# Softmax denominators of an attention stage: through memory as rows, in place of TensorE transposes

## The chip, the cores and the metric

The kernel runs on one core of one Trainium2 chip. The metric is the device time of one execution in microseconds (us), taken as the median of several runs. The engines are named as the profile names them: PE (TensorE, with PEld for its weight loads), DVE (VectorE), ACT (ScalarE), POOL (GpSimd) and SP (SyncE, which here issues nearly all DMAs).

## What is computed

Two layers of a trunk with 1024 latent tokens and 256 context tokens, D = 1024. Each layer projects the normalised input, runs three token mixers (retention with 4 heads, grouped-query attention with 6, latent attention "MLA" with 6), multiplies the concatenated heads by a SiLU gate and projects back:

```python
def block_attention(q, k, v, scale):      # gqa: 6 heads; mla: 6 heads, with a rotary part in q and k
    s = einsum('bqkgd,bskd->bkgqs', qi, k) * scale
    p = softmax(s, axis=-1)
    return einsum('bkgqs,bskd->bqkgd', p, v)

def _post(x, o_ret, o_gqa, o_mla, z_gate, g_res, w_out):
    y = concatenate([o_ret, o_gqa, o_mla], axis=-1) * silu(z_gate)
    return x + g_res * (y @ w_out)
```

The part at issue is the softmax's division by the sum of the exponentials, which the kernel does after the product with V, and the product with the gate.

## The kernel before, in words

All is float32, with operands of matmuls split into a high and a low part. Tokens lie in 10 tiles of 128 (8 latent, 2 context). A layer is a projection stage, an attention stage and an output projection. The attention stage is at about 520 to 1000 us in the first layer and 1570 to 2036 us in the second.

The attention stage works on pairs: `Pair(i, pr, mla)` is one head i (0 to 5) of one kind (mla 1, or grouped-query 0) and two neighbouring query tiles 2 pr and 2 pr + 1 (pr 0 to 4). There are 30 pairs of each kind per layer. Their order is the list `pairs` (L1391 to L1402): the grouped-query pair x, and the MLA pair x - 3, by turns. A latent pair (pr 0 to 3) has keys in 3 blocks of 512, a context pair (pr 4) one block of 256; each pair has a job per tile and block.

`advance` (L1365) is one step: it writes one s_job (scores, two or three matmuls, then a maximum on DVE), and, some steps later, exp_job (exponentials on ACT, with the row sums; after the last block DVE makes the reciprocals `ri`, L1277 to L1280), t_job (four transposes on PE, copied out by ACT and subtracted by DVE), and pv_job (products with V on PE, summed in one PSUM bank `o`, and added by DVE into the columns of the head, L1317). `clock` counts the steps. The result lies transposed: partition 64 mla + c is channel c of the head, and the free axis is the queries. Grouped-query heads fill partitions 0 to 63, MLA heads 64 to 127 of the same columns, `head_cols(p)` (L1326). The queries were in these columns before.

The reciprocals `ri` lie the other way, with queries on partitions: 128 x (2 tiles x 2 kinds). So `y_job` (L1350), which runs once when both kinds of a head and tile pair are done, copies them on POOL 64 times each into `rb` (L1355), transposes `rb` on PE into a PSUM bank of tag `tp` (L1358; these banks, two of them, serve t_job too), lets DVE multiply (L1359), and POOL multiply by the gates `gt` (L1360), which SP loaded from memory (L1335).

The program is laid out by a planner: the kernel writes instructions with priorities (`up(...)`), and the planner places them on each engine in order of its own estimate of readiness. Each engine then runs its list in order. SP's list holds all loads of the stage: the rotary queries `qst` (L1180, split by POOL into Qr), the gates, the staging `st` of K and V (L1086 to L1107, split by POOL, L192 and L193), and at the end the output weights (L223).

Of the kernel before, what the change touches and what calls it, by code (L numbers as in the profile page):

```python
# [10 lines left out]
F32 = mybir.dt.float32  # L11
# [3 lines left out]
ALU = mybir.AluOpType  # L15
# [3 lines left out]
P = 128  # L19
# [4 lines left out]
DEPTH = 2  # L24
# [52 lines left out]
SV = 0  # L77
WG = 1
PO = 1


def hybrid_trunk(tc, I, O):
# [3 lines left out]
    V, A, G, T = nc.vector, nc.scalar, nc.gpsimd, nc.tensor  # L86
    dma = nc.sync.dma_start
# [12 lines left out]
    s_mv = [tc.dram_tile([6 * P, NCH * 64], F32, name=f"s_mv{l}") for l in range(DEPTH)]  # L100
    s_kpT = [tc.dram_tile([NCH * 32, P], F32, name=f"s_kpT{l}") for l in range(DEPTH)]
    s_mt = [tc.dram_tile([P, 512], F32, name=f"s_mt{l}") for l in range(DEPTH)]
    s_gate = [tc.dram_tile([2, D], F32, name=f"s_gate{l}") for l in range(DEPTH)]


# [6 lines left out]
    ident = cst.tile([P, P], F32, name="ident")  # L112
# [21 lines left out]
    def bank(tag):  # L134
        if tag == "o":
            return pp.tile([P, 512], F32, name=tag, tag=tag, bufs=1)
        if tag == "m":
            tag = "tp"
        bufs = {"acc": NACC, "tp": 7 - NACC}[tag]
        return pp.tile([P, 512], F32, name=tag, tag=tag, bufs=bufs)  # L140

    def up(offset):
        return tc.high_priority(offset=offset) if offset else nullcontext()
# [297 lines left out]
    def phase_b(l, p1, acts, ws, first, first_side, first_done, att):  # L441
# [260 lines left out]
        blk(gqa_fn, post=side)  # L702
        blk(gqb_fn, post=side, posts=PO)
        for _ in side:
# [355 lines left out]
    def attention(l, att):  # L1060
# [3 lines left out]
        at = None  # L1064
# [174 lines left out]
        exps, trs, pvs, ys = [], [], [], []  # L1239
        clock = [0]  # L1240
# [27 lines left out]
        def exp_job(p, i, b, ps):  # L1268
            pn = at.tile([P, 512], F32, name="pn", tag="pn", bufs=PN)[:, :p.w]
            A.activation(pn, ps, AF.Exp, bias=p.ng[i], accum_out=p.su[:, i, b:b + 1])  # L1270
            p.pn[i, b] = pn
            if b == p.nb - 1 and i == 1:
                if (p.i, p.pr) not in ris:
                    ris[p.i, p.pr] = sm.tile([P, 2, 2], F32, name="ri", tag="ri", bufs=RB)
                ri = ris[p.i, p.pr][:, :, p.mla]
                if p.nb > 1:
                    V.tensor_reduce(ri, p.su[:, :, 0:p.nb], axis=AX.X, op=ALU.add)  # L1277
                    V.reciprocal(ri, ri)
                else:
                    V.reciprocal(ri, p.su[:, :, 0])  # L1280

        def t_job(p, i, b):
            if i == 0:
# [42 lines left out]
        def head_cols(p):  # L1326

            return yxs[:, 2 * p.pr:2 * p.pr + 2, Y_H + p.i * 128:Y_H + (p.i + 1) * 128]

        ris, halves, gates = {}, {}, {}  # L1330
# [8 lines left out]
        def gate_retention(p):  # L1339
# [5 lines left out]
            if p.i == 1:  # L1345
                rets.append((p.pr, at.tile([P, 2, 2, 128], F32, name="gr", tag="gr", bufs=1)))
                dma(rets[0][1].rearrange("p k t c -> p k (t c)"),
                    s_gT[l][0:Y_H, 2 * p.pr * P:(2 * p.pr + 2) * P].rearrange("(k p) c -> p k c", p=P))

        def y_job(p):  # L1350

            pm = bank("tp")[:, :256]
            ri = ris.pop((p.i, p.pr)).rearrange("p t s -> p (t s)")
            rb = at.tile([P, 256], F32, name="rb", tag="rb", bufs=1)
            G.tensor_scalar(rb.rearrange("p (x c) -> p x c", c=64), ri.unsqueeze(2).to_broadcast([P, 4, 64]), 1.0, 1.0,  # L1355
                            op0=ALU.mult, op1=ALU.mult)
            for i in range(2):
                T.transpose(pm[:, i * 128:(i + 1) * 128], rb[:, i * 128:(i + 1) * 128], ident)  # L1358
            V.tensor_tensor(head_cols(p), head_cols(p), pm.rearrange("p (t c) -> p t c", t=2), op=ALU.mult)  # L1359
            G.tensor_tensor(head_cols(p), head_cols(p), gates.pop((p.i, p.pr)), op=ALU.mult)  # L1360
            gate_retention(p)

        LAG_E, LAG_T, LAG_V = LE, LT, LV
# [1 line left out]
        def advance(jobs):  # L1365

            s = clock[0]
            if jobs is not None:
                with up(OS):
                    s_job(*jobs)  # L1370
            if exps and s >= LAG_E:
                with up(OE):
                    exp_job(*exps.pop(0))
            if trs and trs[0][0] <= s and (trs[0][2], trs[0][3]) in trs[0][1].pn:
                _, p, i, b = trs.pop(0)
                with up(OT):
                    t_job(p, i, b)
                if i == 1:
                    h = max(1, p.nch // HV)
                    pvs.append((s + LAG_V, p, b, 0, h))  # L1380
                    pvs.append((s + LAG_V + 1, p, b, h, p.nch))
            if pvs and pvs[0][0] <= s:
                with up(OV):
                    pv_job(*pvs.pop(0)[1:])
            if ys and ys[0][0] <= s:
                with up(OY):
                    y_job(ys.pop(0)[1])
            clock[0] += 1
# [3 lines left out]
        for x in range(30 + LEAD):  # L1392
            for mla, y in ((1, x - LEAD), (0, x)):
                if 0 <= y < 30:
                    p = Pair()
# [20 lines left out]
        for n, p in enumerate(pairs):  # L1416
# [7 lines left out]
            for u in range(2):  # L1424
                for b in range(p.nb):
                    if early[0] == 0:
                        yield "prepared"
                        at = att.ctx.enter_context(tc.tile_pool(name=f"at{l}", reuse_waits="tile", bufs=1))
# [18 lines left out]
                    if credit[0] >= 1:  # L1447
                        credit[0] -= 1
                        step()
        while exps or trs or pvs or ys:  # L1450
            advance(None)
        att.ctx.close()

# [239 lines left out]
```

## Time and profile before

| | us |
|---|---|
| median of 3 runs | 2163.22 (2162.13 to 2165.7) |
| the profiled execution | 2162.85 |
| its span | 2161.1 |
| PE busy | 2084.2 (96%) |
| PE weight loads busy | 1870.0 (87%) |
| DVE busy | 1502.0 (70%) |
| ACT busy | 1183.5 (55%) |
| POOL busy | 978.2 (45%) |

Busy shares are averages over stages of different kinds. A stage is read from its windows (busy time of each engine in a stretch), its waits (who stood idle for whom) and its timeline (instructions by start). Durations of matmuls overlap with their neighbours, so that the time a matmul takes of PE is better read from the start of the next one.

### The profile page before, as it was taken

Reading aid. Unit: us, or ns where it says so; the run is one execution under the profiler, and the core shown is the slowest. Engines: PE = TensorE matmul, PEld = TensorE weight load, DVE = VectorE, ACT = ScalarE, POOL = GpSimd, SP = SyncE. Lnnn points to the kernel's source line nnn. Section 1 sums busy time; section 2 is a strip of 40 time slices with the busy share of each in tenths; the row PEclk is TensorE's granted clock in tenths of the full one; section 3 lists DMA queues with packets and bytes.
Section 4 is the critical chain, followed back from the end, with each engine's and each line's share of the span. In section 5 each row is a group of like instructions: output and inputs, shape, how many; then the busy total and the mean of one; then the engine's idle time right before and its main releaser. Section 6 shows DMA issues by size and latency. Waiting matters only on the chain. (4 is left out here: it accounts for less than half of the span.)

```text
span 2161.1 us, 42292 instructions
## 1 busy us (share of the span) xinstructions
PE 2084.2 (96%) x14888; PEld 1870.0 (87%) x14888; DVE 1502.0 (70%) x3830; ACT 1183.5 (55%) x3180; POOL 978.2 (45%) x1444
## 2 busy tenths in 40 slices
PE   7999999999999999999999999998999999999998
PEld 3899987788888888888999999887788888888898
DVE  4625583666889999997174358546689899999824
ACT  3503333225788888886243233322488888888623
POOL 2341242315576465533543324233375656453474
PEclk8999999999999999999999999999999999999999
DMA  9542446414111010004143212452311111000322
GB/s 315 145 145 63 123 112 204 122 49 117 36 44 28 20 30 25 13 27 136 46 153 102 66 54 55 140 152 66 109 46 30 32 30 32 14 22 18 98 91 98
DMA packets 189117, 173.30 MB, mean 80 GB/s; under 512 B 35833, under 2 KB 171625, under 8 KB 188905
## 3 DMA queue, kind: packets, MB, share of 16 engines
q1 hardware_dynamic: 187464, 165.35, 25.7%
q10 hardware_dynamic: 1440, 5.24, 0.6%
q8 instruction: 119, 1.95, 0.4%
q14 instruction: 94, 0.76, 0.1%
HBM read 124.77 MB, written 45.76 MB: 79 GB/s over the span
## 5 line engine op out<-in xcount | busy, mean ns | idle before, releaser
L256 PE MATMUL acc<-wh,ah 128*128 128x256 f32 (+1 forms) x1760 | 503.4, 286 | 1.8 <-ACT ah L404 1.8
L258 PE MATMUL acc<-wh,al 128*128 128x256 f32 (+1 forms) x1760 | 500.6, 284 | 2.5 <-DVE al L405 2.4
L257 PE MATMUL acc<-wl,ah 128*128 128x256 f32 (+1 forms) x1760 | 502.7, 286 | 0.0
L1256 DVE TENSOR_REDUCE nm<-acc 128x1 f32<-128x512 f32 (+1 forms) x624 | 411.7, 665 | 39.0 <-PE acc L1250 27.0
L1293 DVE TENSOR_TENSOR pT<-tp,pT 128x512 fp32r<-128x512 f32 (+1 forms) x624 | 413.2, 664 | 36.1 <-ACT pT L1292 30.6
L1292 ACT CAST pT<-tp 128x512 fp32r<-128x512 f32 (+1 forms) x624 | 356.5, 573 | 139.1 <-PE tp L1288 132.8
L1270 ACT ACTIVATE pn<-acc,nm 128x512 f32<-128x512 f32 (+1 forms) x624 | 421.3, 681 | 19.9 <-DVE nm L1261 17.4
L1288 PE MATMUL tp<-ident,pn 128*128 128x128 f32 x2400 | 424.1, 274 | 3.9 <-DVE pT L1293 2.4
L256 PEld LDWEIGHTS acc<-wh,ah 128*128 128x128 f32 x1760 | 334.9, 190 | 13.1 <-issue 8.2
L258 PEld LDWEIGHTS acc<-wh,al 128*128 128x128 f32 x1760 | 332.0, 189 | 5.3 <-DVE al L405 4.5
L257 PEld LDWEIGHTS acc<-wl,ah 128*128 128x128 f32 x1760 | 334.0, 190 | 0.8 <-issue 0.8
L1304 PE MATMUL o<-pT,V 128*128 128x256 f32 x1200 | 326.3, 294 | 0.7 <-DVE yx L1317 0.6
L1288 PEld LDWEIGHTS tp<-ident,pn 128*128 128x128 f32 x2400 | 287.6, 140 | 34.6 <-PE tp L1288 5.8
L1305 PE MATMUL o<-pT,V 128*128 128x256 f32 x1200 | 314.4, 284 | 0.0
L1304 PEld LDWEIGHTS o<-pT,V 128*128 128x128 f32 x1200 | 227.1, 189 | 19.2 <-DVE yx L1317 5.1
L1305 PEld LDWEIGHTS o<-pT,V 128*128 128x128 f32 x1200 | 227.2, 189 | 16.6
L192 POOL TENSOR_SCALAR wh<-raw 128x512 fp32r<-128x512 f32 (+2 forms) x144 | 82.4, 582 | 321.2 <-PE acc L258 143.2
L193 POOL TENSOR_TENSOR wl<-raw,wh 128x512 fp32r<-128x512 f32 (+2 forms) x144 | 164.7, 1155 | 5.2
L1247 PE MATMUL acc<-K,Qm 128*128 128x512 f32 (+1 forms) x312 | 140.6, 451 | 1.0
L683 PE MATMUL acc<-ah,wh 128*128 128x512 f32 (+1 forms) x384 | 141.4, 368 | 0.0
L684 PE MATMUL acc<-ah,wl 128*128 128x512 f32 (+1 forms) x384 | 139.8, 364 | 0.0
L685 PE MATMUL acc<-al,wh 128*128 128x512 f32 (+1 forms) x384 | 139.5, 363 | 0.0
(278 smaller groups left out, 3898.3 us busy)
## 6 DMA issues: line engine op xcount, KB each, us to landing
raw<-in_w_ada_dram SPq DMA_DIRECT2D x96, 256.0 KB, 3.2
raw<-in_w_in_dram SPq DMA_DIRECT2D x56, 256.0 KB, 2.9
kv<-s_rkv SPq DMA_DIRECT2D x40, 256.0 KB, 2.8
s_gT<-eo SPq DMA_DIRECT2D x80, 128.0 KB, 2.2
yx<-in_x_sample_dram SPq DMA_DIRECT2D x16, 512.0 KB, 6.4
gt<-s_gT SPq DMA_DIRECT2D x60, 128.0 KB, 2.1
raw<-in_w_in_dram SPq DMA_DIRECT2D x56, 128.0 KB, 2.5
raw<-in_w_out_dram SPq DMA_DIRECT2D x48, 128.0 KB, 3.0
```

Source lines behind the costliest of these rows:

```text
L193: G.tensor_tensor(wl, raw, wh.bitcast(F32), op=ALU.subtract)
L256: T.matmul(ps, ah[:, k, :], wh, start=(k == 0), stop=False)
L257: T.matmul(ps, ah[:, k, :], wl, start=False, stop=False)
L258: T.matmul(ps, al[:, k, :], wh, start=False, stop=(k == KC - 1))
L683: T.matmul(ps, wh, ah[:, k, :], start=(k == 0), stop=False)
L1256: V.tensor_reduce(nm[:, b:b + 1], ps, axis=AX.X, op=ALU.max, negate=True)
L1270: A.activation(pn, ps, AF.Exp, bias=p.ng[i], accum_out=p.su[:, i, b:b + 1])
L1288: T.transpose(pt[:, c * 128:(c + 1) * 128], pn[:, c * 128:(c + 1) * 128], ident)
L1292: A.copy(ph, p3)
L1293: V.tensor_tensor(pl, p3, ph.bitcast(F32), op=ALU.subtract)
L1304: T.matmul(p.po, vc, p.gran[b][:, 0, c, :], start=(ch == 0), stop=False)
L1305: T.matmul(p.po, vc, p.gran[b][:, 1, c, :], start=False, stop=(ch == last))
```

## The change

The reciprocals of a pair go to a new memory tile `s_sum`, 128 queries x 4 sums, transposed by the access pattern of the store (`r q -> q r`), right after the MLA part's reciprocals; three steps of `clock` later `load_sums` writes two loads, each of which brings one kind's row of sums to 64 partitions (the row is read 64 times). `y_job` multiplies these rows into the gates on POOL, and the gates into the head's columns on POOL. The POOL copy, the two PE transposes with their PSUM bank, and the DVE product are gone. `rb` has two buffers in place of one.

```diff
--- before.py
+++ after.py
@@ -77,6 +77,7 @@
 SV = 0
 WG = 1
 PO = 1
+SL = 3
 
 
 def hybrid_trunk(tc, I, O):
@@ -100,6 +101,7 @@
     s_mv = [tc.dram_tile([6 * P, NCH * 64], F32, name=f"s_mv{l}") for l in range(DEPTH)]
     s_kpT = [tc.dram_tile([NCH * 32, P], F32, name=f"s_kpT{l}") for l in range(DEPTH)]
     s_mt = [tc.dram_tile([P, 512], F32, name=f"s_mt{l}") for l in range(DEPTH)]
+    s_sum = [tc.dram_tile([120, P], F32, name=f"s_sum{l}") for l in range(DEPTH)]
     s_gate = [tc.dram_tile([2, D], F32, name=f"s_gate{l}") for l in range(DEPTH)]
 
 
@@ -1278,6 +1280,9 @@
                     V.reciprocal(ri, ri)
                 else:
                     V.reciprocal(ri, p.su[:, :, 0])
+                if p.mla:
+                    dma(sums_of(p).rearrange("r q -> q r"), ris.pop((p.i, p.pr)).rearrange("p t s -> p (t s)"))
+                    rows_due.append((clock[0] + SL, p))
 
         def t_job(p, i, b):
             if i == 0:
@@ -1347,17 +1352,24 @@
                 dma(rets[0][1].rearrange("p k t c -> p k (t c)"),
                     s_gT[l][0:Y_H, 2 * p.pr * P:(2 * p.pr + 2) * P].rearrange("(k p) c -> p k c", p=P))
 
+        def sums_of(p):
+
+            x = 4 * (5 * p.i + p.pr)
+            return s_sum[l][x:x + 4, :]
+
+        rows_due, srows = [], {}
+
+        def load_sums(p):
+
+            srows[p.i, p.pr] = rb = at.tile([P, 2, 128], F32, name="rb", tag="rb", bufs=2)
+            for s in range(2):
+                dma(rb[64 * s:64 * s + 64], sums_of(p).rearrange("(t s) q -> s t q", s=2)[s:s + 1].to_broadcast([64, 2, 128]))
+
         def y_job(p):
 
-            pm = bank("tp")[:, :256]
-            ri = ris.pop((p.i, p.pr)).rearrange("p t s -> p (t s)")
-            rb = at.tile([P, 256], F32, name="rb", tag="rb", bufs=1)
-            G.tensor_scalar(rb.rearrange("p (x c) -> p x c", c=64), ri.unsqueeze(2).to_broadcast([P, 4, 64]), 1.0, 1.0,
-                            op0=ALU.mult, op1=ALU.mult)
-            for i in range(2):
-                T.transpose(pm[:, i * 128:(i + 1) * 128], rb[:, i * 128:(i + 1) * 128], ident)
-            V.tensor_tensor(head_cols(p), head_cols(p), pm.rearrange("p (t c) -> p t c", t=2), op=ALU.mult)
-            G.tensor_tensor(head_cols(p), head_cols(p), gates.pop((p.i, p.pr)), op=ALU.mult)
+            g = gates.pop((p.i, p.pr))
+            G.tensor_tensor(g, g, srows.pop((p.i, p.pr)), op=ALU.mult)
+            G.tensor_tensor(head_cols(p), head_cols(p), g, op=ALU.mult)
             gate_retention(p)
 
         LAG_E, LAG_T, LAG_V = LE, LT, LV
@@ -1382,6 +1394,8 @@
             if pvs and pvs[0][0] <= s:
                 with up(OV):
                     pv_job(*pvs.pop(0)[1:])
+            if rows_due and rows_due[0][0] <= s:
+                load_sums(rows_due.pop(0)[1])
             if ys and ys[0][0] <= s:
                 with up(OY):
                     y_job(ys.pop(0)[1])
@@ -1447,7 +1461,7 @@
                     if credit[0] >= 1:
                         credit[0] -= 1
                         step()
-        while exps or trs or pvs or ys:
+        while exps or trs or pvs or rows_due or ys:
             advance(None)
         att.ctx.close()
```

## Rows read from the trace of the kernel before

**Rows 1.** Windows: stretch, length, busy of PE, PEld, DVE, ACT, POOL, clock, DMA.

```profile
665.93:744.69 78.76, 78.48 (x541) 69.34 (x540) 72.19 (x154) 65.80 (x167) 44.03 (x72) 1.00 0.10 25
744.69:823.40 78.71, 78.41 (x541) 69.31 (x540) 72.11 (x154) 65.84 (x167) 44.00 (x72) 1.00 0.09 26
```

**Rows 2.** Timeline of PE at three L1358: start, duration, instruction, count.

```profile
726.00 0.28 PE L1247 MATMUL acc<-K,Qg 128*128 128x256 f32 x1
726.12 0.28 PE L1248 MATMUL acc<-K,Qg 128*128 128x256 f32 x1
726.48 0.41 PE L1358 MATMUL tp<-ident,rb 128*128 128x128 f32 x2
726.90 0.38 PE L1304 MATMUL o<-pT,V 128*128 128x256 f32 x1
727.13 0.28 PE L1305 MATMUL o<-pT,V 128*128 128x256 f32 x1
...
744.50 0.39 PE L1248 MATMUL acc<-K,Qg 128*128 128x512 f32 x1
744.73 0.38 PE L1358 MATMUL tp<-ident,rb 128*128 128x128 f32 x2
745.01 0.38 PE L1304 MATMUL o<-pT,V 128*128 128x256 f32 x1
745.23 0.28 PE L1305 MATMUL o<-pT,V 128*128 128x256 f32 x1
745.35 0.28 PE L1304 MATMUL o<-pT,V 128*128 128x256 f32 x1
...
756.98 0.40 PE L1247 MATMUL acc<-K,Qg 128*128 128x512 f32 x1
757.24 0.41 PE L1358 MATMUL tp<-ident,rb 128*128 128x128 f32 x2
757.40 0.48 PE L1248 MATMUL acc<-K,Qg 128*128 128x512 f32 x1
757.72 0.32 PE L1304 MATMUL o<-pT,V 128*128 128x256 f32 x1
```

**Rows 3.** Waits of PE for rb: total us, times, longest us.

```profile
PE tp L1358 <- POOL rb L1355: 9.9, 6, 3.2
```

**Rows 4.** Windows, the stretch behind the first long wait.

```profile
564.70:568.20 3.50, 3.40 (x15) 3.30 (x16) 1.35 (x3) 0.33 (x1) 3.07 (x7) 0.51 0.00 1
```

**Rows 5.** Timeline of DVE, first layer's drain; idle before in brackets.

```profile
998.92 0.42 DVE L1317 TENSOR_TENSOR yx<-o,o 64x256 f32<-64x256 f32 x1 [0.84 <-POOL yx L1360]
```

**Rows 6.** Groups of instructions by line: busy us, mean ns, idle before.

```profile
L1360 POOL TENSOR_TENSOR yx<-yx,gt 128x256 f32<-128x256 f32 x60 | 44.4, 740 | 11.8 <-DVE yx L1359 5.8 <-issue 3.1
...
L1359 DVE TENSOR_TENSOR yx<-yx,tp 128x256 f32<-128x256 f32 x60 | 25.2, 421 | 10.1 <-PE tp L1358 8.1
...
L1355 POOL TENSOR_SCALAR rb<-ri 128x256 f32<-128x256 f32 x60 | 24.4, 407 | 82.9 <-PE tp L1358 45.1 <-DVE ri L1278 23.2 <-DVE yx L1317 7.5
```

**Rows 7.** DMA issues by line: count, KB each, median us to landing.

```profile
gt<-s_gT SPq DMA_DIRECT2D x60, 128.0 KB, 2.1
...
s_gkT<-koT SPq DMA_DIRECT2D x20, 64.0 KB, 1.5
...
mcos<-in_mcos_dram SPq DMA_DIRECT2D x2, 128.0 KB, 3.8
```

**Rows 8.** Timeline, one rb on POOL, and its transposes on PE.

```profile
602.61 0.41 POOL L1355 TENSOR_SCALAR rb<-ri 128x256 f32<-128x256 f32 x1 [2.71 <-DVE ri L1278]
...
613.91 0.41 PE L1358 MATMUL tp<-ident,rb 128*128 128x128 f32 x2
```

**Rows 9.** Waits of SP's queue, the longest in total.

```profile
SPq L1180 <- POOL Qr L193: 347.7, 50, 13.3
```

**Rows 10.** Waits of POOL, the longest in total.

```profile
POOL Qm L1169 <- PE acc L1248: 186.6, 34, 7.4
```

**Rows 11.** Windows, POOL splitting the next head's K and V.

```profile
625.00:650.00 25.00, 21.72 (x154) 19.45 (x154) 20.44 (x44) 18.27 (x46) 18.61 (x27) 1.00 0.21 56
```

## Prediction

> **What bounds the kernel now.** I read the busy shares by slice on the page first, then the stretches by windows, then the waits. The change lies wholly inside the two attention stages (about 520 to 1000 us and 1570 to 2036 us, from the first and last start of L1358 and L1247), so only those count. The steady unit is a group of five query-tile pairs, four latent and one context, for one head of each kind; it repeats every 78.7 us [rows 1]. In it PE is idle 0.3 us, DVE 6.5, ACT 13 and POOL 35 (span minus busy). So TensorE sets the pace, DVE comes next with 92% busy, and POOL, to which the change moves work, has 44% to spare. A busy row does not prove a full engine, since matmul times overlap. So I take starts instead: score matmuls of 256 columns start 0.12 us apart, PV matmuls 0.12, and a step from one kind to the next leaves no hole [rows 2]. PE issues back to back; what is taken out of its stream shortens the stage.
>
> **What leaves PE.** y_job runs 60 times (30 per layer), with two transposes each. Their printed durations overlap with their neighbours, so I price them by the starts around them [rows 2]. Base: 0.12 for a matmul of 256 columns, twice that (0.24) for a score matmul of 512.
> First place (two of five in a group): L1248 starts at 744.50, the PV matmul behind the transposes at 745.01 and the next at 745.23: 0.73 us, where 0.24 + 0.12 would do. Price 0.37. Second (two of five): 756.98 to 757.72, 0.74 us where two score matmuls take 0.48: 0.26. Third (one of five, a context pair): 726.12 to 727.13, 1.01 where 0.24 would do: 0.77. Mean of five: (2 x 0.37 + 2 x 0.26 + 0.77) / 5 = 0.41. Six y_jobs (three per layer) fall into the drain at the end of a stage and are counted there. 54 x 0.41 = 22 us.
> PE also stood waiting for POOL's rb: 9.9 us in six waits, the longest 3.2 [rows 3]. Four of these are over 1 us (two per layer, where POOL is late). PE is what bounds the stage, so they go in full; nothing else on PE waits for y_job. Behind the first of them the granted clock was 0.51 over 3.5 us, its lower level of 1.2 GHz [rows 4]; before it fell, PE had stood still. That stretch costs 3.5 x 0.49 = 1.7 us, and goes with the wait.
> In the drain at the end of each layer DVE runs L1317, then L1359, then the splits that the output projection waits for; it also waited 0.84 us there for POOL [rows 5]. Without L1359 (0.42 us [rows 6]) the drain is shorter by something between 0 and 2 us per layer; I take 1 each, one L1359 and part of that wait: 2 us.
> Sum: 22 + 9.9 + 1.7 + 2 = 35.6 us.
>
> **What leaves or moves elsewhere.** DVE loses 60 x 0.42 = 25 us and keeps all else; it stays behind PE (72 - 5 x 0.42 = 70 us of a group that shrinks to about 76.7). POOL loses L1355 (0.407 mean) and gets a product of gate and rows, which I price as L1360 (0.74, same shape, two inputs from SBUF) [rows 6]: +0.33 x 60 = 20 us, 1.7 per group, against 35 idle. Hidden by that idle time; without the cover, 20 us. One PSUM bank of tag tp is no longer taken by y_job, which can only free L1288.
>
> **What comes in on SP.** Three DMAs per pair: a store of 128 x 4 sums in pieces of 4 bytes, and two loads of rows for 64 partitions each. The store waits on SP for the reciprocal, the loads for the store's landing and for the buffer of two pairs before; behind them on SP are the query rope loads (qst), gates (gt), K and V staging, and at the end of the layer the output weights. Each of these is then held by at most the chain. No row has such a store. Bounds: 1.5 us to landing, as the store of 128 pieces of 512 bytes (koT), and 3.8, as the load of 1024 pieces of 128 bytes (mcos) [rows 7]. I take 2.1, near the first, since it has half as many pieces as mcos and 1/64 of its bytes. The loads are like gt, 2.1. Chain: 3.6 to 5.9 us, 4.2 taken. Is that covered? One reciprocal was ready when POOL started rb at 602.61, and the transposes that used it ran at 613.91: 11.3 us [rows 8]. So the rows are there before they are wanted, with over 5 us to spare. SP itself stood waiting most of the stage (347.7 us for POOL's Qr alone) [rows 9], so 4 us more per 15.7 us is no load. If the cover were gone, POOL would stand the remainder of it, and behind it the Q and K splits would be late; POOL made most Qm as soon as PE let a buffer go (186.6 us of waiting for that) [rows 10], so it works ahead of need. I put the cost at 0, between -1 us (nothing here but a shorter queue speaks for a gain) and the slow case below.
>
> The Trainium skill (Perfetto Trace Analysis, section Identifying the Most-Contended Engine) says that matmul busy time says little of how near TensorE is to its limit and that the share of weight loads does. Here that share is 69.3 of 78.7 us, 88%, so by this rule TensorE would have 12% to spare, and the sum would be far smaller; the starts of matmuls [rows 2] speak against it.
>
> **Sum.** Profiled execution 2162.85 us (span 2161.1); less 35.6 is 2127. The planner will place a changed list of instructions and set some new waits; I leave 3 us for that, a choice: the size of the longest wait it left PE this time. 2130, which against the median of 2163.22 is -1.5%.
>
> **Rivals.**
> DVE becomes the bound. It is 92% busy, and in stretches of grouped-query jobs more. Then the freed PE slots turn into waits for DVE, and only the waits and the clock come back: 2162.85 - 9.9 - 1.7 = 2151. Against: DVE loses 0.42 where PE loses 0.41, so their distance stays as it is.
> Nothing comes back. If PE had room (the weight-load view), or if the planner's new order put as much waiting elsewhere, the time stays at about 2163. Against: 0.3 us of PE idle in 78.7.
> Slower: POOL stands at the rows. POOL is in order, and the product can be placed as early as the old rb was, right behind the reciprocal [rows 8]; then it would wait the whole chain, 3.6 to 5.9 us per pair. Where a head changes (K and V of the next are split) POOL has 6.4 us idle in 25 [rows 11], with 25 / 15.7 = 1.6 pairs: 4.0 per pair. Above a wait of 4.0 per pair, POOL falls behind there, and Qr or K come late to PE. Price: ten head changes, two pairs in each, a stall like the longest wait (3.2 us [rows 3]) at each: 64 us, net of the forecast's gain 2130 + 64 = 2194. Against: Q parts are made ahead, and the product's place follows the landing that the planner expects.
> The store is slow by its shape. If 512 pieces of 4 bytes took over 15.7 - 2.1 = 13.6 us to land, rows would come slower than pairs and each further us would cost 60: at 15 us, 2130 + 84 = 2214. Against: 3.8 us for twice the pieces [rows 7]. The Trainium skill (VectorE: DVE Perf Modes, section The three transpose paths) warns of just this: a plain DMA that transposes by strides is 19 times slower than the hardware's transposing DMA, which it gives as 1309 ns for 128 x 128; an estimate from that page is 25 us for a full tile, and here a 32nd of one is moved. By the page's full figure this rival would hold; no row before the change shows such a store.
>
> **How the numbers follow.** Forecast (2118 to 2142): 66%. DVE bound, or half of it (2142 to 2158): 14%. Nothing back: 7%. POOL stands: 10%. Slow store: 3%. 0.2%, 4.3 us, is about what a measurement of this kernel can tell from no change. Faster 0.80, same 0.07, slower 0.13. Range 2118 to 2158: its low end is the sum with no allowance for the planner, all of the drain (4 us), and 7 us for waits of DVE and L1288 that go too; its high end takes in the second case. The first and second hold 8 in 10.
>
> **What would show it.** No L1358 in the trace and groups of five at 76.7 us; fewer than 1 us of PE waiting for POOL in both stages; granted clock 1.00 around 565 us; the store landing between 1.5 and 3.8 us; POOL waiting for DMA at the new product for less than 1 us per pair, and no wait of PE on Qr, Q or K. A group still at 78.7 with DVE at full share would be the second case; POOL waiting 4 us and more per pair with PE waiting on Qr or K, the slow one.

## The result, and the profile after

The changed kernel takes 2395.88 us (median) where the kernel before takes 2162.68 beside it: 1.107 times as long, 95% interval 1.104 to 1.109. Slower by 233 us, where 33 us less was forecast. One of its four runs took 2981.96 us at a mean granted clock of 0.62, and the ratio and its interval go by the other three. The profiled execution took 2392.99 us.

The first rows are from the page: the span, the busy times, and, by engine, the share of the span that the chain of work that ended last can be followed through.

```profile
span 2391.2 us, 42335 instructions
PE 2131.5 (89%) x14768; PEld 1906.2 (80%) x14768; DVE 1478.5 (62%) x3770; ACT 1183.3 (49%) x3180; POOL 990.7 (41%) x1444
...
PE 13%; DMA 10%; POOL 6%; DVE 2%; issue 1%; SPq 1%; ACT 0%; POOLq 0%; ACTq 0%; DVEq 0%
```

TensorE lost 120 matmuls, as the change says, and is nevertheless busy for longer than before and idle for 260 us. In the chain DMA stands with 10% of the span; before, it stood with 1%. In the code after, the lines of interest are L1284 (the store of the sums), L1366 (the loads of the rows), L1371 and L1372 (POOL's products, with the rows and with the gates), L1182 (the loads of the rotary queries `qst`), L194 and L195 (their split into `Qr`) and L1171 and L1173 (the query parts `Qg` and `Qm`). The waits (total us, times, longest us) of TensorE, POOL and SP, the largest that the change touches (L258 is the output projection at the end of a layer, L406 the split of its input):

```profile
PE acc L1249 <- POOL Qg L1171: 130.9, 20, 15.8
PE acc L1250 <- POOL Qg L1173: 16.5, 27, 1.1
PE acc L258 <- ACT ah L406: 23.3, 4, 10.9
POOL gt L1371 <- DMA rb<-s_sum: 467.8, 50, 14.9
SPq L1366 <- DMA s_sum<-ri: 439.5, 58, 9.3
SPq L1182 <- POOL Qr L195: 253.0, 44, 8.2
```

TensorE's 9.9 us of waiting for `rb` [rows 3] are gone, and 147 us of waiting for POOL's query parts stand there instead. POOL, which used to wait for TensorE [rows 10], waits 468 us for the rows; SP waits 440 us for the store. In windows of 25 us (stretch, length, busy time of PE, PEld, DVE, ACT, POOL, granted clock, DMA share, GB/s) from 700 to 1025 us every second one has a hole:

```profile
575.00:600.00 25.00, 25.00 (x175) 22.16 (x174) 23.27 (x49) 21.92 (x57) 11.33 (x20) 1.00 0.09 15
...
775.00:800.00 25.00, 25.00 (x161) 22.10 (x161) 21.33 (x45) 19.47 (x49) 7.11 (x12) 0.92 0.06 14
800.00:825.00 25.00, 18.18 (x113) 15.69 (x112) 14.71 (x32) 13.87 (x37) 9.00 (x16) 0.86 0.13 20
825.00:850.00 25.00, 24.96 (x174) 22.25 (x173) 22.63 (x48) 21.32 (x54) 18.18 (x28) 1.00 0.21 43
850.00:875.00 25.00, 16.34 (x99) 13.90 (x98) 12.77 (x28) 12.22 (x33) 11.05 (x18) 0.85 0.12 30
```

Before, five pairs ran without a hole [rows 1]. With the holes comes the lower clock: 0.85 and 0.86 in the two windows in which TensorE stood, and 0.92 in the window from 775 us, in which it was busy throughout and yet made 161 matmuls, where the window from 825 us at 1.00 has 174.

What holds the pair up is seen in the timelines of SP and of POOL over one turn (start, duration, engine, line, instruction; in brackets the idle time before it and what ended it):

```profile
583.12 0.38 SPq L1284 DMA_DIRECT2D s_sum<-ri  x1
591.51 1.24 SPq L1366 DMA_DIRECT2D rb<-s_sum  x2
599.87 0.79 SPq L1182 DMA_DIRECT2D qst<-s_qrT  x2
600.77 0.38 SPq L1284 DMA_DIRECT2D s_sum<-ri  x1
...
673.92 0.59 SPq L1284 DMA_DIRECT2D s_sum<-ri  x1
...
772.50 0.38 SPq L1284 DMA_DIRECT2D s_sum<-ri  x1
```

```profile
595.23 0.74 POOL L1371 TENSOR_TENSOR gt<-gt,rb 128x256 f32<-128x256 f32 x1 [11.77 <-DMA rb<-s_sum]
596.06 0.89 POOL L1171 TENSOR_SCALAR Qm<-yx 64x256 fp32r<-64x256 f32 x2
597.01 1.53 POOL L1173 TENSOR_TENSOR Qm<-yx,Qm 64x256 fp32r<-64x256 f32 x2
...
599.11 0.73 POOL L195 TENSOR_TENSOR Qr<-qst,Qr 64x256 fp32r<-64x256 f32 x1
```

Read it as a ring. The store goes out at 583.12, and the loads that wait for it at 591.51, 8.4 us later. 3.7 us after them the rows are there and POOL, which had stood 11.77 us, makes its product (595.23). Behind that product in POOL's list are the next query parts; the last of them, `Qr`, ends at 599.84. At 599.87 SP issues the loads of `qst`, which had waited for that `Qr` to free their buffer, and the next store, which lies behind them in SP's list, at 600.77. Then it begins again. One turn, from store to store, is 600.77 - 583.12 = 17.65 us (8.4 + 3.7 + 4.6 + 0.9). TensorE needs 78.7 us for a group of five pairs of each kind [rows 1], 15.7 us a pair on the mean. This turn is one of the shortest, and TensorE is still full beside it (the window from 575 us). Five turns in a row, one group, take 772.50 - 673.92 = 98.6 us, 19.7 each: in some of them the next store also lies behind a gates' load, which waits for POOL's second product (L1372) to free a buffer (61.5 us of such waits on SP in all). So TensorE runs out of queries twice in a group, and then no engine is full and each waits for another in turn.

The lists of stores (duration in ns, first and last start in us) give the size of the loss; the first two are the changed kernel's layers, the last two those of the run with a plain store, told below, which has the same matmuls and no hole:

```profile
L1284 SPq DMA_DIRECT2D s_sum<-ri x30: 376/384/679, 563.1 to 1102.3; - x30
L1284 SPq DMA_DIRECT2D s_sum<-ri x30: 378/384/1095, 1720.7 to 2256.7; - x30
```

```profile
L1284 SPq DMA_DIRECT2D s_sum<-ri x30: 320/378/584, 561.1 to 970.7; - x30
L1284 SPq DMA_DIRECT2D s_sum<-ri x30: 319/382/1793, 1586.6 to 1994.9; - x30
```

From the first to the last store it is 539.2 and 536.0 us, against 409.6 and 408.3: 257 us more, nearly all of the 265 us between the two spans. From store to store it is 18.5 us on the mean of both layers, (539.2 + 536.0) / 58, instead of 14.1 (both means hold the last pairs of a layer, whose stores follow each other faster).

### The profile page after: what moved, and what is told of

Same layout as the page of the kernel before. It is cut to its first block, busy times and chain, and to the rows that moved or that the text cites. A ratio compares the mean times of both kernels' runs of the same rounds, so it can differ in the third digit from the quotient of the medians.

```text
span 2391.2 us, 42335 instructions
## 1 busy us (share of the span) xinstructions
PE 2131.5 (89%) x14768; PEld 1906.2 (80%) x14768; DVE 1478.5 (62%) x3770; ACT 1183.3 (49%) x3180; POOL 990.7 (41%) x1444
## 2 busy tenths in 40 slices
DMA packets 238076, 181.29 MB, mean 76 GB/s; under 512 B 69432, under 2 KB 220584, under 8 KB 237864
## 5 line engine op out<-in xcount | busy, mean ns | idle before, releaser
L258 PE MATMUL acc<-wh,ah 128*128 128x256 f32 (+1 forms) x1760 | 509.0, 289 | 29.4 <-ACT ah L406 23.3
L1293 PE MATMUL tp<-ident,pn 128*128 128x128 f32 x2400 | 449.6, 280 | 3.1 <-DVE pT L1298 2.4
L258 PEld LDWEIGHTS acc<-wh,ah 128*128 128x128 f32 x1760 | 340.4, 193 | 41.6 <-ACT ah L406 24.1
L259 PEld LDWEIGHTS acc<-wl,ah 128*128 128x128 f32 x1760 | 339.4, 193 | 3.1 <-POOL wl L195 2.2
L1309 PE MATMUL o<-pT,V 128*128 128x256 f32 x1200 | 337.5, 302 | 1.8 <-DVE yx L1322 1.8
L1293 PEld LDWEIGHTS tp<-ident,pn 128*128 128x128 f32 x2400 | 298.1, 143 | 35.0 <-PE tp L1293 6.3
L1310 PE MATMUL o<-pT,V 128*128 128x256 f32 x1200 | 323.8, 290 | 0.0
L1371 POOL TENSOR_TENSOR gt<-gt,rb 128x256 f32<-128x256 f32 x60 | 44.7, 746 | 563.9 <-DMA rb<-s_sum 467.8
L1249 PE MATMUL acc<-K,Qg 128*128 128x512 f32 (+1 forms) x300 | 145.5, 485 | 132.2 <-POOL Qg L1171 130.9
L1309 PEld LDWEIGHTS o<-pT,V 128*128 128x128 f32 x1200 | 238.8, 199 | 18.7 <-DVE yx L1322 4.4
L1310 PEld LDWEIGHTS o<-pT,V 128*128 128x128 f32 x1200 | 237.9, 198 | 18.8
L194 POOL TENSOR_SCALAR wh<-raw 128x512 fp32r<-128x512 f32 (+2 forms) x144 | 81.1, 573 | 322.5 <-PE acc L260 143.6
L1249 PEld LDWEIGHTS acc<-K,Qg 128*128 128x128 f32 x300 | 62.5, 208 | 139.8 <-POOL Qg L1171 135.6
L195 POOL TENSOR_TENSOR wl<-raw,wh 128x512 fp32r<-128x512 f32 (+2 forms) x144 | 162.1, 1137 | 5.2
L1250 PE MATMUL acc<-K,Qg 128*128 128x512 f32 (+1 forms) x300 | 145.8, 488 | 16.8 <-POOL Qg L1173 16.5
```

What stands on the lines that cost most here:

```text
L195: G.tensor_tensor(wl, raw, wh.bitcast(F32), op=ALU.subtract)
L258: T.matmul(ps, ah[:, k, :], wh, start=(k == 0), stop=False)
L259: T.matmul(ps, ah[:, k, :], wl, start=False, stop=False)
L1249: T.matmul(ps, p.Q[:, 0, qs], K, start=True, stop=False)
L1293: T.transpose(pt[:, c * 128:(c + 1) * 128], pn[:, c * 128:(c + 1) * 128], ident)
L1309: T.matmul(p.po, vc, p.gran[b][:, 0, c, :], start=(ch == 0), stop=False)
```

## The experiments

The theory after the first look at this trace: the ring decides, and it is longer than TensorE's pair because the store lands late by its shape, 512 pieces of 4 bytes. Rivals: SP is the bound by its standing; POOL's waiting costs by itself, wherever the product stands; the store is slow for the number of its pieces; the loads are what is slow.

Each experiment is one run, but for e8 (four runs). In e2, e4, e6, e7, e9 and e12 the rows that come back to POOL are not the reciprocals of the pair, so these price a store or a wait; of the kernels near 2130 us only e8 computes what the kernel before does.

| run | us | span |
|---|---|---|
| before, beside them | 2160 to 2162 | |
| after | 2395.88 | 2391.2 |
| e1, product with the rows last | 2203.11 | 2201.3 |
| e2, store not turned | 2128.07 | 2126.3 |
| e3, store and loads, unused | 2176.00 | 2174.1 |
| e4, loads wait for no store | 2149.11 | 2147.3 |
| e5, store issued from ACT | 2236.18 | 2234.2 |
| e6, pieces 64 bytes apart | 2133.09 | 2131.3 |
| e7, half the pieces | 2436.15 | 2434.4 |
| e9, pieces 16 bytes apart | 2129.05 | 2127.3 |
| e12, pieces 8 bytes apart | 2136.92 | 2135.1 |
| e11, one more buffer for `qst` | 2387.42 | 2385.6 |
| e8, sums turned on DVE | 2129.35 | 2127.9 |

### The store not turned (e2)

```diff
-dma(sums_of(p).rearrange("r q -> q r"), ris.pop(...).rearrange("p t s -> p (t s)"))
+dma(sums_of(p).rearrange("r (a b) -> (r a) b", b=4), ris.pop(...).rearrange("p t s -> p (t s)"))
```

> The changed kernel with the store of the sums in 128 pieces of 16 bytes, not turned (memory holds them query by query), and the loads unchanged; so the rows that come back are not those of the reciprocals, and the output is not the reference's. It prices the store's shape. If the 8.4 us to landing come from 512 pieces of 4 bytes, the landing falls to about 2 us, a turn of the ring to 4.6 + 0.9 + 2 + 3.6 = 11 us, below PE's 15.7: 2125 to 2160 us, and POOL stands under 2 us per pair. If the landing is what any store that a load waits for takes, it stays at 8 us and the time at about 2390.

2128.07 us. The same 2 KB go to the same place as 128 pieces of 16 bytes. From its page, its waits, and its DMA issues (count, KB each, median us to landing):

```profile
PE 2059.6 (97%) x14768; PEld 1853.5 (87%) x14768; DVE 1487.4 (70%) x3770; ACT 1177.5 (55%) x3180; POOL 998.6 (47%) x1444
```

```profile
POOL gt L1371 <- DMA rb<-s_sum: 141.9, 36, 7.4
...
SPq L1366 <- DMA s_sum<-ri: 74.8, 54, 3.4
```

```profile
s_sum<-ri SPq DMA_DIRECT2D x60, 2.0 KB, 2.2
```

With a landing of 2.2 us the whole loss is gone and the gain of the removed work is there: the span is 34.8 us shorter than before. POOL still stands 142 us at its product, and no wait of TensorE for POOL's query parts is left among its waits: POOL's standing cost nothing here, where the ring's turn is shorter than the pair. In instruction stream, loads and products the kernel is the changed one, so the rival that the loads are slow falls.

The Trainium skill (DMA: Bandwidth & Descriptors, section Rules for kernel authors) says that an access whose last dimension is not contiguous becomes one descriptor for each element, and advises to rearrange it. The traces agree in the count: by their pages, packets under 512 bytes are 69432 in the changed kernel and 46392 in this one, a difference of 23040 = 60 x (512 - 128).

### Store and loads, with nobody waiting (e3), and loads that wait for no store (e4)

e3 is the kernel before, with the store and the loads of the change added and their rows read by nobody:

```diff
+                if p.mla:
+                    dma(sums_of(p).rearrange("r q -> q r"), ris[p.i, p.pr].rearrange("p t s -> p (t s)"))
+                    rows_due.append((clock[0] + SL, p))
...
+            rw = at.tile([P, 2, 128], F32, name="rw", tag="rw", bufs=1)
+            for s in range(2):
+                dma(rw[64 * s:64 * s + 64], sums_of(p)...)
```

> The kernel before, with the store and the two loads added in the places of the change (one buffer for the rows), and nobody reads the rows: POOL, PE and DVE work as before. Rival SP: SP stands 8 us per pair for the store, and qst, gates, K and V behind it come late: 2163 plus 100 to 230 us. Ring or rival POOL: nothing waits for the rows, so 2160 to 2185 us.

2176.00 us, 14 us above before.

```profile
SPq L1366 <- DMA s_sum<-ri: 436.4, 53, 11.0
...
PE tp L1376 <- POOL rb L1373: 23.0, 6, 10.1
```

SP stands just as long as in the changed kernel (436.4 and 439.5 us) and that costs 14 us: TensorE's wait for `rb` grows from 9.9 us [rows 3] to 23.0, which is 13 of them. What SP's standing costs is thus known, and it isn't 233 us.

In e4 all is as in the changed kernel, but the loads read a constant and needn't wait for the store, which is still made:

```diff
-dma(rb[64 * s:64 * s + 64], sums_of(p).rearrange(...)...)
+dma(rb[64 * s:64 * s + 64], I["ident"][0:4, :].rearrange(...)...)
```

> The changed kernel, but the loads read rows of a constant in memory, so that they wait for no store (which is still made); the output is not the reference's. It takes the landing out of the chain and leaves everything else, and so measures what the removal of the transposes and of the DVE product gives: by the sum of the prediction 2127 to 2140 us; if DVE were the bound, about 2151; if PE's slots were not what bounds, 2163.

2149.11 us, 21 above the plain store's and a little over what was expected.

```profile
POOL gt L1371 <- DMA gt<-s_gT: 82.0, 27, 9.7
...
PE acc L1249 <- POOL Qg L1171: 9.9, 2, 7.5
```

The ring is gone with the wait for the store. What is left is that the gates' load, a plain one of 128 KB that lands in 2.1 us in the kernel before [rows 7], now has POOL waiting for it, up to 9.7 us. One such load on SP, the store just before it, and the product on POOL that waited for the load:

```profile
582.62 0.38 SPq L1284 DMA_DIRECT2D s_sum<-ri  x1
583.09 0.46 SPq L1340 DMA_DIRECT2D gt<-s_gT  x1
...
592.03 0.74 POOL L1371 TENSOR_TENSOR gt<-gt,rb 128x256 f32<-128x256 f32 x1 [7.04 <-DMA gt<-s_gT]
```

The load is issued 0.47 us behind the slow store and is there 8.9 us later. The gates' load before it, issued at 574.88 with no store just ahead, had POOL's product start at 577.11, 2.2 us later.

### Cutting the ring elsewhere (e1, e5, e11)

If a ring decides, cutting any of its links must give most of the loss back while the store stays as slow as it is. In e1 POOL makes the product with the rows last in the pair, into the head's columns:

```diff
-            g = gates.pop((p.i, p.pr))
-            G.tensor_tensor(g, g, srows.pop((p.i, p.pr)), op=ALU.mult)
-            G.tensor_tensor(head_cols(p), head_cols(p), g, op=ALU.mult)
+            G.tensor_tensor(head_cols(p), head_cols(p), srows.pop((p.i, p.pr)), op=ALU.mult)
+            G.tensor_tensor(head_cols(p), head_cols(p), gates.pop((p.i, p.pr)), op=ALU.mult)
```

> The changed kernel with one edit: POOL multiplies the rows into the head's columns (after PV) and then the gates, instead of rows into gates. The store, its 4-byte pieces and both loads stay. Theory 1, a ring: POOL's product waits for the rows, Qr stands behind the product on POOL, the qst load waits on SP for Qr, the next store stands behind qst, and lands 8.4 us later; one turn is about 4.6 + 0.9 + 8.4 + 3.6 = 17.5 to 19 us per pair against 15.7 that PE needs. Here the product is wanted only after PV, some 11 us after the reciprocals, so Qr is no longer behind a wait for rows: expected 2130 to 2180 us, with the wait of SP for the store still at 7 to 8 us each. Rival SP: SP's standing at the loads for the store's landing is what costs, by late qst and K loads: then this stays above 2300. Rival POOL: POOL's standing alone costs, wherever the store stands in SP's list: also 2130 to 2180 here.

2203.11 us: 193 us come back, 23 fewer than the least expected.

```profile
POOL yx L1370 <- DMA rb<-s_sum: 253.0, 37, 14.9
SPq L1366 <- DMA s_sum<-ri: 415.3, 55, 9.7
PE acc L1249 <- POOL Qg L1171: 20.2, 2, 10.2
...
PE acc L258 <- ACT ah L406: 27.2, 4, 13.2
```

```profile
650.00:675.00 25.00, 15.77 (x90) 13.52 (x91) 11.72 (x25) 10.55 (x28) 18.00 (x30) 0.80 0.21 47
675.00:950.00 275.00, 271.65 (x1864) 240.82 (x1863) 248.22 (x522) 229.49 (x585) 154.92 (x246) 0.99 0.16 32
```

SP's wait for the store is hardly shorter; TensorE's wait for `Qg` falls from 130.9 to 20.2. POOL, now asked later, still stands for rows 253 us, but behind the first head change, from 675 to 950 us, TensorE is full at clock 0.99: there the ring is cut. The 75 us that e1 takes more than e2 lie elsewhere. They are at the first head change of a layer (in the first from 650 us) and at the end of a layer, where the output projection waits 27.2 us for columns that POOL has still to multiply by rows. That second wait is there in the changed kernel too (23.3 us) and is no ring; in e2, where the store lands early, it is 1.8 us.

In e5 the store is issued from ACT, so it no longer lies behind the `qst` loads in SP's list:

```diff
-                    dma(sums_of(p).rearrange("r q -> q r"), ...)
+                    A.dma_start(sums_of(p).rearrange("r q -> q r"), ...)
```

> The changed kernel with one word different: the store of the sums is issued from ACT's queue, the loads stay on SP. The store no longer stands behind the queries' load on SP, so it goes out when DVE has the reciprocals. Ring theory (POOL's product waits for rows, the Q parts stand behind it, SP's queries' load waits for them, the next store stands behind that): with the store out of SP's queue the ring has one link less, the turn is what is left of it, 4.6 us on POOL, 0.9 us and the loads' 3.5 us, some 9 us against the 15.7 us that PE needs for a pair. So 2130 to 2180 us, with TensorE's wait for the Q parts under 20 us in sum where the changed kernel has 130.9. Rival (the store's 8 us of landing alone, or POOL's standing by itself, makes the loss, whatever queue the store is in): the same 8 us stand between reciprocals and rows, and the time stays at 2300 us or more. Rival three (ACT stands at the store for DVE's reciprocal): ACT would lose some 0.5 us in each of 60 pairs, up to 30 us, and the waits of TensorE for ACT grow.

2236.18 us, between the two: neither 2180 nor 2300. The windows show why.

```profile
625.00:650.00 25.00, 8.82 (x63) 7.75 (x61) 8.97 (x19) 6.87 (x18) 16.70 (x26) 0.73 0.21 59
...
775.00:800.00 25.00, 25.00 (x177) 22.46 (x176) 23.11 (x50) 21.11 (x56) 13.79 (x22) 1.00 0.11 17
...
850.00:875.00 25.00, 24.32 (x170) 21.42 (x169) 22.52 (x48) 20.45 (x55) 12.49 (x20) 1.00 0.16 28
```

```profile
PE acc L1249 <- ACT pn L1272: 42.5, 10, 20.3
...
ACT pn L1272 <- DMA st<-s_kv: 38.1, 2, 20.9
ACT pT L1297 <- DMA rb<-s_sum: 19.5, 4, 9.0
```

From 775 to 875 us, where the changed kernel has a hole in every second window, TensorE is busy 24.3 us or more in each window, at clock 1.00, and no wait for `Qg` is left among its waits: the ring is cut. POOL still stands 301 us for rows, so the rival that its standing costs by itself falls. The price is new: ACT, which has TensorE's exponentials to make, stands at its store, 38.1 us in two places, and TensorE behind it (the window from 625 us); shorter stands of the same kind, 19.5 us and others, come near the start and the end of a layer. The profile names loads of V and of rows as what ended them; why a store on ACT's queue waits for them is not settled.

In e11 `qst` got a third buffer (and `rb` one instead of two, for the room):

```diff
-rb = at.tile([P, 2, 128], F32, name="rb", tag="rb", bufs=2)
+rb = at.tile([P, 2, 128], F32, name="rb", tag="rb", bufs=1)
...
-st = at.tile([P, 256], F32, name="qst", tag="qst", bufs=2)[0:64]
+st = at.tile([P, 256], F32, name="qst", tag="qst", bufs=3)[0:64]
```

> The changed kernel with its store as it is; only the link of the ring between POOL and SP is cut: the queries' loads have three buffers instead of two, so that SP's load need not wait for the Q part that POOL has still to split, and the next store behind it goes out earlier. To find the room the rows have one buffer instead of two. Ring theory: a load for two pairs on waits for a Q part that was done a pair ago, the store goes out when the reciprocals are there, and what is left per pair is 8.1 us of landing and 3.5 us of loads on SP, under 15.7: 2130 to 2210 us, with TensorE's wait for the Q parts under 30 us in sum where the changed kernel has 130.9. Rival (the landing itself, or POOL's standing for rows, makes the loss without any ring): 2350 us or more. Against the theory: with one buffer of rows SP's load also waits for POOL's product of the pair before, which is another link between the same two queues; if that link decides, 2300 us or more with SP's wait for POOL's product in the place of its wait for the Q part.

2387.42 us. It cut nothing, and so tells nothing against the ring:

```profile
SPq L1182 <- POOL Qr L195: 247.2, 43, 9.1
```

That wait is as long as with two buffers (253.0). SP loads `qst` as soon as a buffer is free; with three it loads three MLA pairs ahead instead of two, and so still waits for the newest `Qr` each time.

### What makes the store slow (e7, e6, e9, e12)

All four have the changed kernel's products and number of loads, and other addresses in memory for the store. e7 stores two of the four sums of each query, 256 pieces, and its loads read each row twice; e6, e9 and e12 store all 512 pieces of 4 bytes, 64, 16 and 8 bytes apart:

```diff
-dma(sums_of(p).rearrange("r q -> q r"), ris.pop(...).rearrange("p t s -> p (t s)"))
+dma(sums_of(p)[0:2].rearrange("r q -> q r"), ris.pop(...).rearrange("p t s -> p (t s)")[:, 0:2])
...
+dma(sums_of(p).rearrange("r (q e) -> q r e", e=16)[:, :, 0], ris.pop(...).rearrange("p t s -> p (t s)"))
```

(e is 4 and 2 in e9 and e12, and the rows of `s_sum` are e times as long; the loads read their first 128 columns, and one more transfer fills `s_sum` before each attention.)

> The changed kernel with half of the store: 256 pieces of 4 bytes instead of 512 (the sums of the first tile alone, which the loads then read for both tiles, so the output is not the reference's). If the landing goes by the number of pieces, with 2.0 us at none, it falls from 8.1 to about 5 us; the ring's turn falls from 17.9 to 14.8 us, which is under the 15.7 us that TensorE needs for a pair, and the time falls by most of the loss, to 2130 to 2230 us. If the landing has a floor of its own for pieces this small, it stays at 7 to 8 us and the time stays above 2330 us.

> The changed kernel, with the 512 pieces of 4 bytes of each store written 64 bytes apart in memory instead of side by side; the loads read another 128 columns of the same rows, so the output is not the reference's, and one more transfer fills the memory once in each attention. If pieces of 4 bytes that fall side by side hold each other up in memory, the store now lands in 2 to 4 us and the time is 2125 to 2200 us. If it is the number of pieces that counts, wherever they fall, the store still lands some 8 us after its issue and the time stays at 2370 to 2420 us. I give the second three chances in four.

> As the run with pieces 64 bytes apart, but 16 bytes apart: four pieces where the changed kernel has sixteen, in the same stretch of 64 bytes (the loads read other columns, the output is not the reference's, and one more transfer per attention fills the memory). Theory (pieces that fall within one short stretch of memory are written one behind the other): the landing, 2.1 us with one piece in a stretch and 8.1 us with sixteen, has some 0.4 us for each piece more, so four of them land in about 3.3 us, and the ring's turn, 17.9 us with 8.1, is 13.1 us, under TensorE's 15.7: 2128 to 2150 us. Rival (only pieces that touch hold each other up, since a gap of any size ends it): 2.0 to 2.2 us of landing and 2125 to 2135 us. Rival (it takes whole 64 bytes of gap): 6 us or more and 2250 us or more.

> As the run with pieces 16 bytes apart, but 8 bytes apart: eight pieces in 64 bytes (the loads read other columns, the output is not the reference's). The landings so far are 2.1 us with one piece in 64 bytes, 2.8 with four and 8.4 with sixteen. If the landing goes by the number of neighbours, eight give 4 to 5.5 us; by the ring, whose turn without the landing is 9.3 us, a landing of up to 6.4 us costs nothing against TensorE's 15.7 us per pair, so the time stays at 2125 to 2150 us. Rival (each further us of landing costs time from the first): 5 us would lie between 2129 and 2396 by its share, about 2230 us. Rival (only pieces that touch hold each other up): landing 2.2 to 2.8 us and 2125 to 2135 us.

Their stores, with the median us to landing, in this order: e7, e6, e9, e12; the last is e11's, whose store is that of the changed kernel.

```profile
s_sum<-ri SPq DMA_DIRECT2D x60, 1.0 KB, 8.6
```

```profile
s_sum<-ri SPq DMA_DIRECT2D x60, 2.0 KB, 2.1
```

```profile
s_sum<-ri SPq DMA_DIRECT2D x60, 2.0 KB, 2.8
```

```profile
s_sum<-ri SPq DMA_DIRECT2D x60, 2.0 KB, 4.4
```

```profile
s_sum<-ri SPq DMA_DIRECT2D x60, 2.0 KB, 8.4
```

I had given the number of pieces three chances in four, and it was wrong. Half as many pieces land no sooner (8.6 us; the kernel is slower still, 2436 us, where its loads, at a median of 4.4 us, also land later than e11's at 3.4). As many pieces with room between them land in 2.1 us, as fast as the plain store. It is where they fall: 1, 4, 8 and 16 pieces in each 64 bytes of memory give 2.1, 2.8, 4.4 and 8.4 us. The rival that only touching pieces count falls with e12. What in the memory puts them one behind the other, and how long the stretch is in which they do so, these runs don't show; the rows of `s_sum` grew longer with the distance, and that was not tried alone.

The time follows the ring and not the landing by its share. Without the landing the turn shown is 17.65 - 8.4 = 9.3 us, so up to a landing of 15.7 - 9.3 = 6.4 us nothing should be lost; by the mean turn of the group from 673.92 us, 19.7 us with a mean landing of 8.5, the limit is 15.7 - 11.2 = 4.5 us. At 4.4 us, over a third of the way from 2.1 to 8.4, the time is 2136.92 us, 8 above the plain store's, where by that share the loss would be 96. Between 4.4 and 8.4 us no run was made, so where the loss begins is not known better.

### The sums turned on DVE (e8)

So the store wants pieces that are long or far apart. Here DVE copies the four columns into a tile of 32 columns of zeros, turns it in blocks of 32 x 32, and the store goes out in four transfers of 4 pieces of 128 bytes.

```diff
+                    rz, rt = rzs[0], at.tile([P, 32], F32, name="rt", tag="rt", bufs=1)
+                    V.tensor_copy(rz[:, 0:4], ris.pop((p.i, p.pr)).rearrange("p t s -> p (t s)"))
+                    V.transpose(rt, rz)
+                    for k in range(4):
+                        dma(sums_of(p)[:, 32 * k:32 * k + 32], rt[32 * k:32 * k + 4])
```

> The changed kernel, but the sums are turned on DVE before they are stored: the four columns are copied into a tile of 32 columns of zeros, turned in blocks of 32 by 32, and stored in four transfers of 4 pieces of 128 bytes each, instead of 512 pieces of 4 bytes. The loads are as they were. DVE gets two small instructions more per pair, SP three issues more. The store should land in about 2 us as in the run with 128 pieces, rows are back 5.5 us after the reciprocals, and the ring has a turn of some 12 us against 15.7. So 2128 us, as in that run, give or take 10: 2120 to 2140 us, faster than the kernel before by 1 to 2%. Rival: three more issues on SP and two more instructions on DVE take it back, 2150 to 2170 us.

2129.35 us against 2161.81 before: 0.986, interval 0.984 to 0.988. It beats both kernels, and has the gain that e2 showed. Its two instructions on DVE (ns min, median, max) and SP's wait for the store:

```profile
L1288 DVE COPY rz<-ri x60: 157/162/927, 548.1 to 1996.8; 128x4 f32<-128x4 f32 x60
L1289 DVE STREAM_TRANSPOSE rt<-rz x60: 192/201/214, 548.8 to 2001.4; 128x32 f32<-128x32 f32 x60
```

```profile
SPq L1373 <- DMA s_sum<-rt: 38.1, 48, 3.4
```

0.36 us of DVE per pair is the price; SP waits 38 us for the store where it waited 440.

## Why the prediction was wrong

**What bounds the kernel: right.** TensorE set the pace, and what left its stream came back. e2 has the changed kernel's matmuls and lacks only the slow landing: its span is 34.8 us shorter, where 35.6 was worked out. PE's busy time fell by 2084.2 - 2059.6 = 24.6 us, where the 54 transposes' slots and the clock were put at 22 + 1.7; the idle time by 10.2 us, where waits and drain were put at 11.9. The weight-load share of 88% spoke for a far smaller gain and was wrong here: at 87% in e2 the gain is there.

**The planner's 3 us, and DVE as the bound: not needed.** The 2128 us of e2 have room for neither.

**The landing of the store: the step that failed first.** Bounded by rows at 1.5 and 3.8 us, taken as 2.1, it was 8.4. Both rows were of other shapes: 512 bytes and 128 bytes a piece. The step took the number of pieces and their bytes as what counts ("half as many pieces as mcos and 1/64 of its bytes"), and neither does. e7 and e6 show it: half the pieces land no sooner, and the same pieces 64 bytes apart land in 2.1 us, the very value taken. No row of before had pieces that lie side by side in memory; the honest end of that range was open at the top.

**"I put the cost at 0" on SP and POOL: the step that made it dear.** With 8.4 + 3.7 = 12.1 us the chain from store to rows is only 0.8 longer than the cover of 11.3 us [rows 8], and by the prediction's own words POOL would stand just the remainder. But the cover was read at the wrong end. It runs from the reciprocal to the transposes on TensorE, and the new reader of the rows is POOL's product. At the turn shown POOL came to that product 0.3 us after the store's issue (595.23 - 11.77 = 583.46, against 583.12) and stood nearly the whole chain. In e2, where the ring costs nothing, it still stood 36 times, 3.9 us each on the mean (141.9 / 36), where the prediction looked for less than 1 us. Missed too was what lies behind the wait. SP's long wait for `Qr` [rows 9] was read as room ("no load"); it is a dependence of SP's list on POOL's. The change added the opposite one, POOL's product on SP's store and loads. Two lists that are run in order and wait for each other make a ring, and a ring has a turn: 17.65 us at the shortest shown and 19.7 on the mean of a group, against 15.7. A late product makes the next store late, so no slack that is read from the kernel before is left in the ring. e3 and e1 separate the two: with the same slow store and nearly the same standing of SP, the kernel loses 14 us where POOL doesn't wait for the rows, and 75 us against e2 where it waits later, with hardly any of it in the steady groups.

**The rivals.** "POOL stands at the rows" had the mechanism nearest to what came: POOL is in order, the product placed early, the query parts late to TensorE. But it looked at head changes only, and priced 64 us with a chain of at most 5.9 us; the stop came in every second window. "The store is slow by its shape" had the cause, at 3%; its deciding point of 13.6 us counted only SP's time per pair. The point by the ring is 4.5 to 6.4 us; e12 (4.4 us, 8 us lost) lies at its lower edge and the changed kernel (8.4) beyond it. The Trainium skill's warning that stood there (VectorE: DVE Perf Modes, section The three transpose paths), that a plain DMA which transposes by strides is 19 times slower than the hardware's when the innermost stride of the destination is large, was the sign to take up, and the row of 1024 pieces of 128 bytes was no answer to it. Its ratio is for another size, and no run here shows it; the same bytes plain and turned are 2.2 and 8.4 us here, a ratio of 3.8. The size of the stride is not what made it slow here: in e6 it is 16 times as large, and the store lands in 2.1 us.

**The clock.** Not foreseen, and a good part of the loss: between e2 and the changed kernel, with the same 14768 matmuls, PE's busy time grows by 2131.5 - 2059.6 = 71.9 us and its idle time by 193. The granted clock was 0.85 where TensorE had stood, and 0.92 in a window behind such a stop, in which it was busy throughout: each stop was paid for again behind it.

## What to carry to other kernels

Before a step goes through memory, write down the list of every engine that it joins and look for a ring: if A's list waits for B and the change makes B wait for A, add up one turn and set it against the pace of the bounding engine; slack read from long waits is no cover for it. A store that scatters neighbouring words of 4 bytes is priced by a row of its own kind or not at all; turn the data on an engine first, so that it goes out in longer pieces (0.36 us on DVE here). Read the cover of a wait at the engine that will do the waiting, and not at the one that did it before. And a profile in which every engine waits and none is full asks for a turn, not for a faster engine.

## What the runs showed of the hardware

- 2 KB in 512 pieces of 4 bytes land in 2.1 us with 64 bytes between their starts, in 2.8 with 16, 4.4 with 8 and 8.4 side by side; 256 pieces side by side take 8.6. The Trainium skill (DMA: Bandwidth & Descriptors, section Latency and other measured facts) gives some 2 us as a DMA's fixed cost; the spread and the plain store agree with that, the side-by-side store does not.
- Such a store holds up what is issued behind it: in e4 a gates' load issued 0.47 us behind it was there 8.9 us after its issue, and POOL waited up to 9.7 us (82 us in sum) for such loads; in the kernel before they land in 2.1 us.
- Moving that store to ACT's queue made ACT stand up to 20.9 us at it (e5), for a reason that is not settled.
